# A normalized tile in two VectorE operations and one of ScalarE, with the first half of three heads in program order

## The chip, the core and the metric

One core of a Trainium2 chip runs the whole program. Its engines are TensorE (matmuls; the profile calls it PE, its weight loads PEld), VectorE (DVE), ScalarE (ACT), GpSimd (POOL) and SyncE (SP, which here only issues DMAs). The metric is the device time of one execution in microseconds, lower is better; a time given is the median of several runs.

## What is computed

A decoder trunk of two layers on 512 tokens of width 1024, all in float32. Each layer is a token mixer (stick-breaking attention in layer 0, a state-space layer in layer 1) and a gated MLP with a causal convolution (the ffn). Ahead of each of these four, and at the end, stands a normalization that is modulated by a conditioning vector:

```python
def rms_norm(x, g):
    y = xf * lax.rsqrt(jnp.mean(xf * xf, axis=-1, keepdims=True) + EPS)
    return y * g
def modulate(h, shift, scale):
    return h * (1 + scale[:, None, :]) + shift[:, None, :]
for i in range(DEPTH):
    h = modulate(rms_norm(x, norm_mix[i]), sh1, sc1)
    x = x + g1 * mixer(h)                    # attention, then state space
    h = modulate(rms_norm(x, norm_ffn[i]), sh2, sc2)
    x = x + g2 * conv_ffn(h, ...)
```

## The kernel before

x lies transposed in SBUF: 8 tiles (k = 0 to 7) of 128 channels by 512 tokens. A matmul in full precision is made of three products (`mm3`): each operand is split in a high part and a low part (hH and hL of the activations, w_h and w_l of the weights), and the products are hH by w_h (L171), hL by w_h (L174) and hH by w_l (L175), all three into one PSUM bank. A weight tile of 128x1024 is split by ScalarE (L165, high) and VectorE (L166, low).

A tile of h is made in `norm_tile`: VectorE multiplies x by rbc, the reciprocal root mean square of each token, broadcast over the partitions (L308, into t); ScalarE makes hH = b + a t (L315, rounded to the matmul's type) and the same once more without rounding into u (L317); VectorE subtracts, hL = u - hH (L321). a and b are columns: one number for each channel. The same function makes tiles 1 to 7 in attention's values stretch (`pinned`, 512 columns, rbc copied into SBUF as rb) and the tiles of three heads.

A head (`head_mm`) is the first part of ffn 0, of the state-space layer and of ffn 1: four banks of output (`hd`; in an ffn, gate and value of units 0 and 1, in the state-space layer u0 to u3) are filled tile by tile while h is being made. For tiles 0 to 5 the tokens are taken in two halves of 256 columns, first all six tiles of the first half, then all six of the second; tiles 6 and 7 are full. The first half can start when the residuals of the first half are complete. While it runs, the tail of the output projection before it finishes the second half: the residual add (L355), its square (L244) and the sum (acc, L245). The second half's statistic (`rstd_stat`: four matmuls L266, ScalarE's root L270, five small VectorE operations L271 to L275 and two diagonal tiles dg, L283) is traced ahead of tile 1's third bank (HEADS = (1, 2)), and its broadcast (`rstd_bc`, L288, a matmul of dg by ones into the bank rbc) ahead of tile 3's third bank (HEADB = (3, 2)).

The order on each engine is set when the program is built: a planner takes instructions that are ready by its own estimate, the earlier traced first, unless an edge says otherwise. `pe_pin` (`keep_in_program_order`) puts an instruction behind the one traced just before it on its engine; it has no say on what is traced later. In `mm3`, `pinned` pins the first of the three products. The products of a bank keep their order among themselves. In the heads the products are not pinned, statistic and broadcast are. `behind_head` queues the splits of the next four weight tiles behind the operations of the head's tiles 4, 8, 11 and 13 (HEADW, places in the list `pin["head"]`).

Behind an ffn's head come the units: for each, two banks of 24 products of 512 columns, then the convolution (ScalarE L459, VectorE L461 twice, for gate and value), Silu (L471), the product (L473) and the split of the result (L477, L478). These follow one another in a written order (`follow`). In ffn 0 VectorE and GpSimd also prepare the tables of the state-space layer in between. In the state-space layer, behind the head, u0 to u3 are copied (L1286) and written to DRAM (sU) and read back in another layout (u); the matmuls pv (L1280) need that.

Of the kernel before, what the change touches and what calls it, by code (L numbers as in the profile page):

```python
# [7 lines left out]
F32 = mybir.dt.float32  # L8
# [3 lines left out]
AF = mybir.ActivationFunctionType  # L12
ALU = mybir.AluOpType
# [3 lines left out]
P = 128  # L17
T = 512
D = 1024
KD = D // P  # L20
# [64 lines left out]
def trunk(tc, I, out, tap=lambda *a: None):  # L85
    with ExitStack() as ctx:
        _trunk(ctx, tc, I, out, tap)


def _trunk(ctx, tc, I, out, tap):  # L90
    nc = tc.nc
    V, S, G, PE, SP = nc.vector, nc.scalar, nc.gpsimd, nc.tensor, nc.sync

    def pool(name, bufs=1, **kw):
        return ctx.enter_context(tc.tile_pool(name=name, bufs=bufs, **kw))
# [5 lines left out]
    np_ = pool("np")  # L101
# [9 lines left out]
    x = [xp.tile([P, T], F32, tag=f"x{k}", name=f"x{k}") for k in range(KD)]  # L111
# [25 lines left out]
    pin = {"head": []}  # L137
# [31 lines left out]
    def mm3(ps, lhs, rhs, start, stop, pinned=False):  # L169
        (ah, al), (bh, bl) = lhs, rhs  # L170
        ins = PE.matmul(ps, ah, bh, start=start, stop=False)  # L171
        if pinned:
            tc.keep_in_program_order(ins)
        PE.matmul(ps, ah, bl, start=False, stop=False)  # L174
        PE.matmul(ps, al, bh, start=False, stop=stop)  # L175
# [7 lines left out]
    def wk(w, k):  # L183
        if isinstance(w[0], list):
            return tuple(half[k // 4][:, k % 4 * P:(k % 4 + 1) * P] for half in w)
        return w[0][:, k * P:(k + 1) * P], w[1][:, k * P:(k + 1) * P]
# [20 lines left out]
    def mcol(l, v, j):  # L207
        return l * 48 + v * 8 + j
# [24 lines left out]
    HALF = (slice(0, T // 2), slice(T // 2, T))  # L233
# [44 lines left out]
    def rstd_stat(R, cr, pinned=False):  # L278
        t0, t1 = cr.start // P, cr.stop // P
        dg = R["dg"]  # L280
        y = rstd_y(R, cr, pinned)
        for i in range(t0, t1):
            ins = V.tensor_scalar(dg[:, i * P:(i + 1) * P], ident, y[:, i - t0:i - t0 + 1], None, ALU.mult)  # L283
        return ins

    def rstd_bc(R, cr, pl, pinned=False):
        bc = bank(pl, "rbc")
        ins = PE.matmul(bc[:, cr], ones, R["dg"][:, cr], start=True, stop=True)  # L288
        if pinned:
            pe_pin(ins)  # L290
        R["bc"][cr.start] = bc
# [7 lines left out]
    def half_cols(ap, cr):  # L299
        return ap.rearrange("p (j c) -> p j c", j=CH)[:, :, cr.start // CH:cr.stop // CH]  # L300

    def norm_tile(h, k, bc, a, b, cr=FULL, pinned=False, first=None, mid=None):
        n = cr.stop - cr.start
        t = np_.tile([P, T], F32, tag="nt1", bufs=2, name="nt1")[:, :n]
        u = np_.tile([P, T], F32, tag="nt2", bufs=1, name="nt2")[:, :n]
        for part in HALF if cr == FULL and isinstance(bc, dict) else (cr,):
            src = bc[part.start] if isinstance(bc, dict) else bc
            pin["nt"] = V.tensor_tensor(t[:, part.start - cr.start:part.stop - cr.start], x[k][:, part], src[:, part], ALU.mult)  # L308
        hh, hl = h[0][k][:, cr], h[1][k][:, cr]
        hf = hh.bitcast(F32)  # L310
        keep = pe_pin if pinned else lambda ins: None
        keep(pin["nt"])
        if first:
            first()
        act = S.activation(hh, t, AF.Identity, bias=b[:, k:k + 1], scale=a[:, k:k + 1])  # L315
        keep(act)
        aff = S.activation(u, t, AF.Identity, bias=b[:, k:k + 1], scale=a[:, k:k + 1])  # L317
        keep(aff)
        if mid:
            mid()  # L320
        dve = V.tensor_tensor(hl, u, hf, ALU.subtract)  # L321
        keep(dve)
        pin["head"].append([act, aff, dve])


    def head_mm(R, h, a, b, hd):
        pin["head"] = []
        todo = [(k, HALF[0]) for k in range(HEADK)] + [(k, HALF[1]) for k in range(HEADK)] + [(k, FULL) for k in range(HEADK, KD)]
        made = 0
        for n, (k, cr) in enumerate(todo):  # L330

            while made < (min(n + 3, HEADK) if cr == HALF[0] else n + 1):
                norm_tile(h, todo[made][0], R["bc"], a, b, todo[made][1])
                made += 1
            for q, (w, ps) in enumerate(hd):
                if cr == HALF[0] and (k, q) == HEADS:
                    rstd_stat(R, HALF[1], True)
                if cr == HALF[0] and (k, q) == HEADB:
                    rstd_bc(R, HALF[1], mm, True)
                mm3(ps[:, cr], wk(w, k), (h[0][k][:, cr], h[1][k][:, cr]), k == 0 and cr.start == 0, k == KD - 1)  # L340

    @contextmanager
    def behind_head(pins=None):
# [82 lines left out]
    def ffn(l, R, prep=None, last=None, hook=lambda: None):  # L426
# [4 lines left out]
        with ExitStack() as fc:  # L431
# [61 lines left out]
            for gi, gn in enumerate(GROUPS):  # L493
# [4 lines left out]
                if gi == 0:  # L498
                    hx, ws = pin["hw"]
                    hd = [(q, s, ws[2 * q + s], bank(name=f"up{l}_{q}_{s}")) for q in range(2) for s in range(2)]  # L500
                    head_mm(R, h, a, b, [q[2:] for q in hd])
                    hx.close()
                    for q in range(4):
                        with behind_head(pin["head"][HEADW[q]]):
                            split_next(False)
                    pin["prep"] = [pin["split"]]
                    for q in range(2):
                        gs.append(unit_out(q, q, [hd[2 * q + s][3] for s in range(2)]))
                    i = 2
                    step = prep(fc) if prep else (lambda: None)  # L510
# [31 lines left out]
    def attention(acc):  # L542
        with ExitStack() as av_, ExitStack() as ac:
# [139 lines left out]
            for k in range(1, KD):  # L683
                def mid():
                    nxt[0] = high(k + 1) if k < KD - 1 else None
                    pe_pin(V.tensor_tensor(w[1], raws[k], w[0].bitcast(F32), ALU.subtract))
                    if k < KD - 1:
                        gv(1, k + 1)

                nxt = [None]  # L690
                gv(0, k)
                norm_tile(h, k, rb, a, mod[:, 0:KD], FULL, True, None, mid)
                if k + 2 < KD:
                    raws[k + 2] = loads(k + 2)
                prods(k, w)
                w = nxt[0]
# [542 lines left out]
    def ssm(R):  # L1239
# [3 lines left out]
        with ExitStack() as zc:  # L1243
# [3 lines left out]
            with ExitStack() as sc:  # L1247
# [20 lines left out]
                hx, ws = pin["hw"]  # L1268
                hd = [(ws[bi], bank(name=f"u{bi}")) for bi in range(4)]
                head_mm(R, h, a, b, hd)  # L1270
                hx.close()
                sp = sc.enter_context(tc.tile_pool(name="ssm", bufs=1, reuse_waits="tile"))
# [211 lines left out]
    b = mod[:, mcol(2, 0, 0):mcol(2, 0, 0) + KD]  # L1484
# [154 lines left out]
```

## Time and profile before

| | us |
|---|---|
| median of 3 runs (1175.2 to 1176.14) | 1175.74 |
| the profiled execution | 1175.82 |
| its span, first to last instruction | 1174.0 |
| TensorE busy | 1158.9 |
| VectorE busy | 857.7 |
| ScalarE busy | 563.5 |

The profile is of one execution. Busy is the time in which an engine has an instruction of its own under way; matmuls are pipelined, a row lasts longer than its turn, and the turn is seen by the distance to the start of the next row. The three heads lie at 262.6 to 290.8 (ffn 0), 634.7 to 658.9 (state space) and 801.6 to 829.8 us (ffn 1); attention's values stretch is 21 to 65 us.

### The profile page before, as it was taken

Reading aid. Unit: us, or ns where it says so; the run is one execution under the profiler, and the core shown is the slowest. Engines: PE = TensorE matmul, PEld = TensorE weight load, DVE = VectorE, ACT = ScalarE, POOL = GpSimd, SP = SyncE. Lnnn points to the kernel's source line nnn. Section 1 sums busy time; section 2 is a strip of 40 time slices with the busy share of each in tenths; the row PEclk is TensorE's granted clock in tenths of the full one; section 3 lists DMA queues with packets and bytes.
Section 4 is the critical chain, followed back from the end, with each engine's and each line's share of the span. In section 5 each row is a group of like instructions: output and inputs, shape, how many; then the busy total and the mean of one; then the engine's idle time right before and its main releaser. Section 6 shows DMA issues by size and latency. Waiting matters only on the chain.

```text
span 1174.0 us, 16592 instructions
## 1 busy us (share of the span) xinstructions
PE 1158.9 (99%) x6242; PEld 964.2 (82%) x6242; DVE 857.7 (73%) x1311; ACT 563.5 (48%) x896; POOL 270.8 (23%) x278
## 2 busy tenths in 40 slices
PE   8999999999999999999999999999999999999997
PEld 7887777699788888888889888789888888888887
DVE  6968888775998666787757599887598378744555
ACT  6756667456453244413346477647443144422443
POOL 2001110000298799979800000000000000000003
PEclk8999999999999999999999999999999999999999
DMA  8873656331267858797756598671176357432322
GB/s 320 292 264 116 192 162 195 111 123 55 78 189 268 247 167 252 198 292 253 230 151 223 149 353 293 207 255 50 49 231 217 107 153 184 133 123 73 92 69 72
DMA packets 91618, 211.01 MB, mean 180 GB/s; under 512 B 19601, under 2 KB 37905, under 8 KB 91538
## 3 DMA queue, kind: packets, MB, share of 16 engines
q1 hardware_dynamic: 78562, 191.08, 51.0%
q0 software_dynamic: 4656, 16.78, 4.5%
q10 hardware_dynamic: 8320, 2.10, 0.8%
q8 instruction: 49, 0.80, 0.3%
q14 instruction: 31, 0.25, 0.1%
HBM read 188.68 MB, written 21.24 MB: 179 GB/s over the span
## 4 chain that ended last, share of the span: by engine, by line
PE 78%; DVE 7%; issue 7%; DMA 5%; ACT 2%; POOL 1%; SPq 1%; POOLq 0%; DVEq 0%; ACTq 0%
PE up L171 13%; PE up L174 13%; PE up L175 13%; PE dn L171 6%; PE dn L174 6%; PE dn L175 6%; DMA wg<-in_w_modT_dram 3%; PE u L174 1%; PE u L171 1%; PE u L175 1%; PE wo L171 1%; PE wos L174 1%; PE wo L175 1%; PE wo L174 1%; PE wos L175 1%
## 5 line engine op out<-in xcount | busy, mean ns | idle before, releaser
L171 PE MATMUL up<-hH,up_h 128*128 128x512 f32 x640 | 249.7, 391 | 0.3 <-DVE ca L461 0.3
L175 PE MATMUL up<-hH,up_l 128*128 128x512 f32 x640 | 249.3, 390 | 0.3 <-DVE up_l L166 0.3
L174 PE MATMUL up<-hL,up_h 128*128 128x512 f32 x640 | 249.3, 390 | 0.0
L461 DVE SCALAR_TENSOR_TENSOR ca<-up,small,ca 128x511 f32<-128x511 f32 (+1 forms) x176 | 131.6, 748 | 120.7 <-ACT ca L459 117.6
L171 PE MATMUL dn<-gH,dn_h 128*128 128x512 f32 (+1 forms) x394 | 145.0, 369 | 0.0
L198 DVE SCALAR_TENSOR_TENSOR wg<-wg,cact 128x1024 f32<-128x1024 f32 x96 | 121.4, 1281 | 31.7 <-DMA wg<-in_w_modT_dram 31.6
L174 PE MATMUL dn<-gL,dn_h 128*128 128x512 f32 (+1 forms) x394 | 144.5, 367 | 0.0
L175 PE MATMUL dn<-gH,dn_l 128*128 128x512 f32 (+1 forms) x394 | 144.4, 366 | 0.0
L171 PEld LDWEIGHTS up<-hH,up_h 128*128 128x128 f32 x640 | 120.1, 188 | 26.5 <-issue 1.5
L175 PEld LDWEIGHTS up<-hH,up_l 128*128 128x128 f32 x640 | 120.1, 188 | 25.9 <-DVE up_l L166 1.1
L174 PEld LDWEIGHTS up<-hL,up_h 128*128 128x128 f32 x640 | 120.1, 188 | 24.4
L459 ACT ACTIVATE ca<-up,small 128x512 f32<-128x512 f32 x88 | 68.2, 775 | 149.5 <-PE up L175 149.5
L1511 POOL TENSOR_SCALAR xa<-x,Anorm_out 128x256 f32<-128x256 f32 x7 | 5.7, 818 | 570.3 <-DVE x L355 570.3
L165 ACT ACTIVATE up_h<-up_r 128x1024 fp32r<-128x1024 f32 x80 | 84.2, 1052 | 75.3 <-PE dn L174 58.1
L166 DVE TENSOR_TENSOR up_l<-up_r,up_h 128x1024 fp32r<-128x1024 f32 x80 | 116.3, 1454 | 5.4 <-ACT up_h L165 4.5
L355 DVE SCALAR_TENSOR_TENSOR x<-dn,mod,x 128x512 f32<-128x512 f32 (+1 forms) x55 | 37.4, 680 | 71.4 <-PE dn L175 71.4
L171 PEld LDWEIGHTS dn<-gH,dn_h 128*128 128x128 f32 x394 | 74.3, 189 | 12.9 <-issue 0.6
L174 PEld LDWEIGHTS dn<-gL,dn_h 128*128 128x128 f32 x394 | 74.3, 189 | 12.1
L175 PEld LDWEIGHTS dn<-gH,dn_l 128*128 128x128 f32 x394 | 74.3, 189 | 12.1
L165 ACT ACTIVATE dn_h<-dn_r 128x1024 fp32r<-128x1024 f32 (+1 forms) x48 | 46.7, 982 | 46.2 <-PE dn L174 38.5
L166 DVE TENSOR_TENSOR dn_l<-dn_r,dn_h 128x1024 fp32r<-128x1024 f32 (+1 forms) x48 | 61.6, 1283 | 0.8 <-ACT dn_h L165 0.5
L477 ACT ACTIVATE gH<-gm 128x512 fp32r<-128x512 f32 x44 | 27.1, 616 | 67.3 <-DVE gm L473 67.3
(349 smaller groups left out, 2311.0 us busy)
## 6 DMA issues: line engine op xcount, KB each, us to landing
up_r<-in_w_up_dram SPq DMA_DIRECT2D x80, 512.0 KB
wg<-in_w_modT_dram SPq DMA_DIRECT2D x71, 512.0 KB
dn_r<-in_w_down_dram SPq DMA_DIRECT2D x32, 512.0 KB
wg<-in_w_modT_dram POOLq DMA_DIRECT2D x25, 512.0 KB, 4.0
wgs<-in_w_modT_dram SPq DMA_DIRECT2D x16, 512.0 KB
dn_r<-in_w_down_dram SPq DMA_DIRECT2D x16, 384.0 KB
wv_r<-in_w_v_dram SPq DMA_DIRECT2D x8, 512.0 KB
wk_r<-in_w_qk_dram SPq DMA_DIRECT2D x8, 512.0 KB
```

The costliest lines, as they stand in the source:

```text
L165: order("S", lambda: S.activation(wh[:, :n], raw[:, :n], AF.Copy))
L166: pin["split"] = order("V", lambda: V.tensor_tensor(wl[:, :n], raw[:, :n], wh[:, :n].bitcast(F32), ALU.subtract))
L171: ins = PE.matmul(ps, ah, bh, start=start, stop=False)
L174: PE.matmul(ps, ah, bl, start=False, stop=False)
L175: PE.matmul(ps, al, bh, start=False, stop=stop)
L198: mul = lambda: V.scalar_tensor_tensor(w, w, 1.0, cact, ALU.mult, ALU.mult, accum_out=raw[:, col:col + 1])
L355: add = lambda: V.scalar_tensor_tensor(xs, pv, gate, xs, ALU.mult, ALU.add)
L459: follow("S", lambda: S.activation(ca, ps, AF.Identity, bias=small[:, cb:cb + 1], scale=tapw[2]))
L461: follow("V", lambda: V.scalar_tensor_tensor(ca[:, q:], ps[:, :T - q], tapw[2 - q], ca[:, q:], ALU.mult, ALU.add))
L477: follow("S", lambda: S.activation(gh, m, AF.Copy))
L1511: G.tensor_scalar(xa[k], x[k][:, cb], a[:, k:k + 1], 0.0, ALU.mult, ALU.add)
```

## The change

The gain a goes into VectorE's first operation, which becomes t = x a rbc; ScalarE makes hH = t + b only; VectorE's second operation adds b itself, hL = (t + b) - hH. The tile u and ScalarE's second operation go. In the heads, the products of the first half (tiles 0 to 5) are traced with `pinned`.

```diff
     def norm_tile(h, k, bc, a, b, cr=FULL, pinned=False, first=None, mid=None):
         n = cr.stop - cr.start
         t = np_.tile([P, T], F32, tag="nt1", bufs=2, name="nt1")[:, :n]
-        u = np_.tile([P, T], F32, tag="nt2", bufs=1, name="nt2")[:, :n]
         for part in HALF if cr == FULL and isinstance(bc, dict) else (cr,):
             src = bc[part.start] if isinstance(bc, dict) else bc
-            pin["nt"] = V.tensor_tensor(t[:, part.start - cr.start:part.stop - cr.start], x[k][:, part], src[:, part], ALU.mult)
+            pin["nt"] = V.scalar_tensor_tensor(t[:, part.start - cr.start:part.stop - cr.start], x[k][:, part], a[:, k:k + 1], src[:, part], ALU.mult, ALU.mult)
         hh, hl = h[0][k][:, cr], h[1][k][:, cr]
-        hf = hh.bitcast(F32)
         keep = pe_pin if pinned else lambda ins: None
         keep(pin["nt"])
         if first:
             first()
-        act = S.activation(hh, t, AF.Identity, bias=b[:, k:k + 1], scale=a[:, k:k + 1])
+        act = S.activation(hh, t, AF.Identity, bias=b[:, k:k + 1])
         keep(act)
-        aff = S.activation(u, t, AF.Identity, bias=b[:, k:k + 1], scale=a[:, k:k + 1])
-        keep(aff)
         if mid:
             mid()
-        dve = V.tensor_tensor(hl, u, hf, ALU.subtract)
+        dve = V.scalar_tensor_tensor(hl, t, b[:, k:k + 1], hh.bitcast(F32), ALU.add, ALU.subtract)
         keep(dve)
-        pin["head"].append([act, aff, dve])
+        pin["head"].append([act, dve])
...
-                mm3(ps[:, cr], wk(w, k), (h[0][k][:, cr], h[1][k][:, cr]), k == 0 and cr.start == 0, k == KD - 1)
+                mm3(ps[:, cr], wk(w, k), (h[0][k][:, cr], h[1][k][:, cr]), k == 0 and cr.start == 0, k == KD - 1, cr == HALF[0])
```

## Rows read from the trace of the kernel before

**Rows 1.** The page, part 1: busy time, share of the span, instructions.

```profile
PE 1158.9 (99%) x6242; PEld 964.2 (82%) x6242; DVE 857.7 (73%) x1311; ACT 563.5 (48%) x896; POOL 270.8 (23%) x278
```

**Rows 2.** Stretches: length, busy of PE, PEld, DVE, ACT, POOL, clock, DMA.

```profile
21.00:62.00 41.00, 41.00 (x185) 33.76 (x184) 38.37 (x58) 30.36 (x53) 0.00 (x0) 1.00 0.85 286
262.50:290.80 28.30, 28.30 (x196) 26.06 (x195) 16.07 (x40) 18.45 (x32) 0.18 (x2) 1.00 0.20 57
```

**Rows 3.** Timeline of TensorE, head 1: start, duration, instruction, how many merged.

```profile
262.59 0.64 PE L171 MATMUL up<-hH,upo_h 128*128 128x256 f32 x4
263.06 0.28 PE L174 MATMUL up<-hL,upo_h 128*128 128x256 f32 x1
...
265.94 0.50 PE L266 MATMUL stat<-ones,acc 128*128 128x1 f32 x4
...
270.17 0.59 PE L288 MATMUL rbc<-dg,ones 128*128 128x256 f32 x2
...
272.49 0.39 PE L171 MATMUL up<-hH,up_h 128*128 128x512 f32 x1
272.87 0.39 PE L174 MATMUL up<-hL,upo_h 128*128 128x256 f32 x1
273.09 0.28 PE L175 MATMUL up<-hH,upo_l 128*128 128x256 f32 x1
```

**Rows 4.** Timeline of ScalarE and TensorE behind head 1, ffn 0.

```profile
289.65 0.78 ACT L459 ACTIVATE ca<-up,small 128x512 f32<-128x512 f32 x1 [6.89 <-PE up L175]
...
307.86 0.39 PE L174 MATMUL up<-hL,up_h 128*128 128x512 f32 x1
308.09 0.39 PE L175 MATMUL up<-hH,up_l 128*128 128x512 f32 x1
308.75 0.47 PE L171 MATMUL up<-hH,up_h 128*128 128x512 f32 x1 [0.27 <-DVE ca L461]
...
309.79 0.50 PE L175 MATMUL up<-hH,up_l 128*128 128x512 f32 x1 [0.34 <-DVE up_l L166]
```

**Rows 5.** Timeline of all engines, start of head 2.

```profile
634.65 0.73 PE L171 MATMUL u<-hH,win_h 128*128 128x256 f32 x4
634.76 0.48 DVE L355 SCALAR_TENSOR_TENSOR x<-dn,mod,x 128x256 f32<-128x256 f32 x1 [0.46 <-PE dn L175]
...
635.16 0.41 DVE L321 TENSOR_TENSOR hL<-nt,hH 128x256 fp32r<-128x256 f32 x1
...
635.63 0.38 PE L174 MATMUL u<-hL,win_h 128*128 128x256 f32 x1 [0.24 <-DVE hL L321]
```

**Rows 6.** Timeline of all engines behind head 2, state-space layer.

```profile
657.68 1.09 ACT L1286 ACTIVATE ut<-u 128x512 f32<-128x512 f32 x2 [3.24 <-PE u L175]
...
668.50 1.15 PE L1280 MATMUL pv<-u,pB 128*64 128x64 f32 x32 [1.30 <-issue]
```

**Rows 7.** ScalarE's groups by form: count, busy, mean ns of one, idle before.

```profile
L317 ACT ACTIVATE nt<-nt,mod,Anorm_ffn 128x256 f32<-128x256 f32 x24 | 14.3, 596 | 0.3 <-DVE hL L321 0.3
L315 ACT ACTIVATE hH<-nt,mod,Anorm_ffn 128x256 fp32r<-128x256 f32 x24 | 14.2, 590 | 4.5 <-DVE nt L308 4.5
...
L244 ACT ACTIVATE sq<-x 128x256 f32<-128x256 f32 x25 | 10.4, 416 | 24.4 <-DVE x L355 22.5 <-DVE acc L245 1.8
```

**Rows 8.** VectorE's groups by form.

```profile
L308 DVE TENSOR_TENSOR nt<-x,rbc 128x256 f32<-128x256 f32 x48 | 18.9, 415 | 2.1 <-PE rbc L288 2.0
...
L321 DVE TENSOR_TENSOR hL<-nt,hH 128x256 fp32r<-128x256 f32 x36 | 15.3, 424 | 7.8 <-ACT nt L317 7.6
...
L355 DVE SCALAR_TENSOR_TENSOR x<-dn,mod,x 128x256 f32<-128x256 f32 x14 | 6.8, 482 | 5.2 <-PE dn L175 5.2
```

**Rows 9.** Timeline of VectorE, head 1, from the statistic to the split.

```profile
267.26 0.43 DVE L321 TENSOR_TENSOR hL<-nt,hH 128x256 fp32r<-128x256 f32 x1
...
267.98 0.48 DVE L283 TENSOR_SCALAR dg<-consts,ny 128x128 f32<-128x128 f32 x2
268.38 1.22 DVE L166 TENSOR_TENSOR up_l<-up_r,up_h 128x1024 fp32r<-128x1024 f32 x1
```

## The prediction

> **What bounds the kernel now.** I read the share of busy time on the page first: TensorE is busy for 1158.9 of 1174.0 us, VectorE for 73%, ScalarE for 48% [rows 1]. So work taken off ScalarE is worth nothing by itself; only a place where TensorE waits can give time back. The table of stretches comes next. In the stretch of the values (21 to 62) TensorE is busy for all 41.00 us, and in the first head (262.5 to 290.8) for all 28.30 [rows 2]. But a matmul's row is longer than its turn: in the head products of 256 columns show 0.28 us and start 0.118 us apart (four from 262.59, the next at 263.06: 0.47/4 [rows 3]), and those of 512 columns show 0.39 and start 0.23 apart (307.86 to 308.09 [rows 4]). Waits shorter than that overlap are therefore no idle time, and I looked for them by the distance of starts, in the timeline of TensorE. Four places are left that this change can touch:
>
> - In heads 1 and 3, at the start of the second half: 272.49 to 272.87 is 0.38 for a product that takes 0.23, and 272.87 to 273.09 is 0.22 for one of 0.12 [rows 3]. That is 0.25 us; head 3 shows the same pattern, so 0.5 for both.
> - In head 2, at its first tile: TensorE starts four products at 634.65 (0.47 of work) and the next one at 635.63, waiting for hL, which VectorE starts at 635.16 because the residual of the tail, 634.76, stands ahead of it [rows 5]. That is 0.98 - 0.47 = 0.51.
> - In the first ffn, 18 us behind head 1: 308.09 to 308.75 instead of 0.23, released by VectorE's convolution (L461, a bank that is not free), and 308.75 to 309.79 for two products (0.46), released by VectorE's weight split [rows 4]. That is 0.43 + 0.58 = 1.0 us. VectorE is behind here since ScalarE could take up the first unit only at 289.65 [rows 4], when the head's first bank was complete.
> - At the first pv of the state-space layer: 1.30 us idle at 668.50, on u0, which goes through DRAM from the copy at 657.68 on [rows 6].
>
> All four together are 3.3 us, and that is about the most that can be had.
>
> **Part 1, the tile of h.** ScalarE loses L317 in each tile: 596 ns in a half tile, 36 of these, and 13 full ones. Its other operation keeps a bias column and loses the scale column; its price lies between 416 ns (the square of the same size, without columns) and 590 as now [rows 7]. I take 500. VectorE's two operations become three-operand forms with a column. The nearest row is the residual L355 of the same size, 482 ns, against 415 and 424 for the forms that go [rows 8]. So each costs between nothing and 67 ns more; I take 67 and 58, as L355 has two tensors and a column like the new ones. Over 55 first and 49 second operations that is at most 55 x 67 + 49 x 58 ns = 6.5 us on VectorE. In the values stretch 7 tiles add 0.9 us to 38.37 of 41.00 [rows 2]; TensorE stays the longer one, so I cost it at nothing, up to +0.1 if the first tile, which TensorE meets at once, is late.
>
> [...]
>
> What counts is the latency from the broadcast to hL. Now: 415 + 590 + about 500 (L317 starts 0.5 behind L315) + 424, some 1.93 us; then: 482 + 500 + 482, some 1.46. hL follows hH after 0.5 instead of 0.95 us. The tile t is now held until hL is made, not until L317 has read it, but both its writer and that reader are VectorE's, so no wait between engines is added. A new wait is that VectorE's first operation needs the gain column, made by ScalarE; in the heads it is made long before. In the values stretch the order written out in the code makes the column one tile ahead, so I cost it at nothing; queued behind that operation would be the split of wv and the next row of the modulation.
>
> **Part 2, the pins.** A pinned instruction is ordered behind the one traced just before it on its engine. With the first product of each bank pinned in the first half, and the three products of a bank in order already, the first half runs bank by bank: statistic ahead of tile 1's third bank, broadcast ahead of tile 3's third. Now the statistic runs at 265.94, behind tile 2's first products, and the broadcast at 270.17, behind all of tile 4 [rows 3]. Then: 18 products from 262.59 give 264.7 for the statistic, and 24 more with its own 0.37 give 267.9 for the broadcast, 2.2 us sooner. The first half ends at about 271.8 (72 x 0.118 + 0.37 + 0.35 behind 262.59; the last two are what statistic and broadcast take out of the row of products now), while hL of the second half's first tile can be there at 267.9 + 0.35 + 0.3 + 1.46 = 270.0. So the waits at 272.5 go; no matmul and no DMA is added or moved between queues.
>
> What TensorE now can't do is pass a late tile: it needs hL one product behind hH, not four, so the 0.45 us gained on hL pays for 0.35 us of sooner need. In head 2 that decides: hH(0) at 634.6, hL at 635.1 if VectorE takes it ahead of the residual, 635.7 if behind. Against 635.6 now: -0.4 or +0.2, and I take 0.
>
> **Where the stall of the ffn goes.** In head 1 TensorE runs 196 instructions in 28.3 us [rows 2], of which the head has 174 (144 half products, 24 full, 4 and 2 for statistic and broadcast). Some 20 are products of unit 2, of 512 columns, the first at 272.49 [rows 3], put where hL was expected late. They take 20 x 0.23 = 4.6 us ahead of the head's last tiles. With hL sooner the order need not hold them, the first unit's bank is complete some 4 us before 289.65, and VectorE's chain of convolutions, which is 1.0 us late 18 us on, begins that much sooner. I take the whole 1.0; if the 20 stay, nothing. What is late next is VectorE's preparation work for the state-space layer, which fills its gaps, and the same total of matmuls.
>
> **At pv.** If the last tile of head 2 runs bank by bank instead of four first products ahead, u0 is complete three products (0.7 us) sooner and the wait of 1.30 shrinks as much; the full tiles are not pinned, so I take 0.3 of 0 to 0.7.
>
> **The sum.** The profiled execution took 1175.82 (span 1174.0 and 1.8 around it); the median of three is 1175.74. Heads 1 and 3: -0.4 of 0.5. Head 2: 0 (-0.4 to +0.2). ffn: -1.0 (0 to -1.0). pv: -0.3 (0 to -0.7). Values: 0 (up to +0.1). Stalls in a strict first half: +0.2 (0 to +1.3 per head, below). Together -1.5: **1174.3 us**.
>
> **Rivals.** *Only the heads tighten* (the 20 products stay, or the pins order nothing that matters): -0.4, 1175.4. For it: the second half and the full tiles are not pinned; against it: the shorter chain holds everywhere. *All four places go*: -0.5 - 0.4 - 1.0 - 0.7 = -2.6, and 0.5 more where products are denser than now: 1172.7. For it: each has hL or the first unit's start as its cause.
>
> *VectorE is late at the broadcast, and TensorE waits with nothing to put in.* Now dg ends 2.52 us behind the statistic (267.98 + 0.48 - 265.94 [rows 3, 9]), with one hL among it. In the strict order TensorE is at the broadcast 3.2 us behind the statistic: 0.7 to spare. The weight split of 1.22 us stands right behind dg now [rows 9], and its ScalarE half comes sooner, too; if it goes ahead of dg, with two tile operations of 0.4 each, dg is 1.22 + 0.8 - 0.7 = 1.3 us late, in three heads 3.9, and the ffn's stall stays: 1179.5 with the 0.2 of the sum in it. It decides from the point where dg ends over 3.2 us behind the statistic.
>
> [...] VectorE is busy for 16.07 of 28.30 us in head 1 [rows 2], so the rows don't call it saturated; the rival needs only a wrong order.
>
> **Chances.** Forecast 0.45, only the heads 0.28, all four 0.17, late broadcast 0.10. A measurement of this kernel tells a change of about 0.2% (2.35 us) from none: faster is below 1173.4, slower above 1178.1. Faster: 0.17 and the lower end of the forecast, 0.10, so 0.27; slower 0.10; the same 0.63. The range takes the all-four case with a little below it (1172.3) and the heads' case with one head stalling by 1.3 (1176.7).
>
> **What would show it.** In the trace after: starts in the first half in the order L171, L174, L175, bank by bank; the statistic near 264.7 and the broadcast near 267.9, with no start more than 0.2 late there; no products of unit 2 ahead of tile 7; the first convolution near 285.5; no wait for VectorE near 308; the wait ahead of pv below 1.3. Wrong it would be if TensorE waits for dg or acc in a head, or if the order of unpinned work elsewhere changes by more than the waits named here.

## The result, and the profile after

The changed kernel takes 1180.88 us (median of five, 1178.6 to 1182.39) against 1175.37 for the kernel before; the ratio is 1.0045, with a 95% interval of 1.0030 to 1.0059. It is 5.3 us slower, where I had forecast 1.5 us faster. The profiled execution has a span of 1179.1 us, 5.1 above the 1174.0 of before.

Line numbers behind ScalarE's operation (L314) are three lower than before (hL is L318, the scan L795, the residual L352). The page's first part says that the work went where I had said, out of ScalarE (563.5 to 532.8) and a little into VectorE (857.7 to 859.7 [rows 1]):

```profile
PE 1161.1 (98%) x6242; PEld 965.6 (82%) x6242; DVE 859.7 (73%) x1311; ACT 532.8 (45%) x847; POOL 271.0 (23%) x278
```

The groups by form, with the mean ns of one behind the comma, give the new prices, to be read beside [rows 7, 8]:

```profile
L314 ACT ACTIVATE hH<-nt,mod 128x256 fp32r<-128x256 f32 x36 | 17.1, 503 | 23.4 <-DVE nt L308 22.3 <-PE wo L175 1.0
L318 DVE SCALAR_TENSOR_TENSOR hL<-nt,mod,hH 128x256 fp32r<-128x256 f32 x36 | 16.4, 482 | 1.1 <-ACT hH L314 1.1
L308 DVE SCALAR_TENSOR_TENSOR nt<-x,Anorm_ffn,rbc 128x256 f32<-128x256 f32 x32 | 14.1, 478 | 2.1 <-PE rbc L288 1.9
L308 DVE SCALAR_TENSOR_TENSOR nt<-x,Amix,rb 128x512 f32<-128x512 f32 x7 | 5.3, 754 | 0.8 <-ACT Amix L583 0.8
```

So the loss is not in the prices: 482 and 500 were forecast, 478 to 482 and 503 are measured. The last row has something that the old tile didn't have, 0.8 us in which VectorE waits for the gain column Amix.

The list of TensorE's waits over the whole span (total us, how many, the longest) shows three places:

```profile
PE t L807 <- DVE om L795: 2.6, 5, 1.0
...
PE rbc L288 <- DVE dg L283: 1.4, 3, 0.6
...
PE stat L266 <- DVE acc L245: 0.8, 2, 0.4
PE u L174 <- DVE hL L318: 0.7, 1, 0.7
```

Before, the second did not occur, the third was 0.3 in one, the fourth 0.2, and the first was this:

```profile
PE t L810 <- DVE om L798: 0.7, 2, 0.5
```

These lists count idle time only; by the distance of starts, TensorE lost 1.8, 2.3 and 1.9 us in the heads against 0.9, 1.2 and 0.9 before, counted from a head's first product on (each sum is the excess over 0.227 us for a product of 512 columns and 0.118 for 256, the distances measured, and over 0.063 for 128, an estimate: half the step of 0.109 between those two, taken off 0.118; the heads have none of 128). Summed in the same way over attention (100 to 244), it lost 17.4 us against 14.0. For the 146 transposes in this stretch the estimate is too low: they start 0.109 us apart, before and after, so that some 6.7 us of each sum (146 x 0.046) are no loss; the 3.4 between them stay. But single executions differ much there: the kernels below whose attention is as before lose 12.3 to 16.9. The wait for the scans (om) is the clearer sign: it is 2.6 here, 3.0 in e1, and at most 1.3 in every other run.

**Attention.** VectorE at the end of the values stretch, after:

```profile
50.10 0.75 DVE L308 SCALAR_TENSOR_TENSOR nt<-x,Amix,rb 128x512 f32<-128x512 f32 x1 [0.36 <-ACT Amix L583]
...
55.41 0.75 DVE L308 SCALAR_TENSOR_TENSOR nt<-x,Amix,rb 128x512 f32<-128x512 f32 x1 [0.47 <-ACT Amix L583]
...
57.21 1.22 DVE L166 TENSOR_TENSOR wk_l<-wk_r,wk_h 128x1024 fp32r<-128x1024 f32 x1
58.35 1.22 DVE L166 TENSOR_TENSOR wq_l<-wq_r,wq_h 128x1024 fp32r<-128x1024 f32 x1
59.48 0.74 DVE L318 SCALAR_TENSOR_TENSOR hL<-nt,mod,hH 128x512 fp32r<-128x512 f32 x1
...
77.22 0.69 DVE L728 TENSOR_TENSOR vn<-vn,vs 128x512 f32<-128x512 f32 x1 [1.31 <-DMA vs<-sV]
...
88.60 5.83 DVE L795 TENSOR_TENSOR_SCAN om<-om,maskb 128x128 f32<-128x128 f32 x8
```

Before, the last hL of the stretch stood ahead of the split wq_l:

```profile
56.73 0.69 DVE L321 TENSOR_TENSOR hL<-nt,hH 128x512 fp32r<-128x512 f32 x1 [0.51 <-ACT nt L317]
57.68 1.23 DVE L166 TENSOR_TENSOR wq_l<-wq_r,wq_h 128x1024 fp32r<-128x1024 f32 x1 [0.26 <-ACT wq_h L165]
...
85.71 5.84 DVE L798 TENSOR_TENSOR_SCAN om<-om,maskb 128x128 f32<-128x128 f32 x8
```

From the first tile on (25.25 before, 25.88 after) hL is 2.1 us later and the scan 2.3. Between them lies a chain. ScalarE's next weight split waits for its load (3.34 us, to 60.93; before 0.79, to 58.43). VectorE's copies of the values out of PSUM stand behind these splits (from 65.94 on, before 63.05). The values are then written to DRAM, read back one row shifted (vs) and subtracted (first at 77.22, before 74.78), and only then do the scans get VectorE. The chain has a little slack: in e2 (below), whose values stretch is as before, hL comes 30.67 us behind the first tile, 0.8 sooner than before, and the scan only 0.2 sooner. At some 114 us TensorE has used up its lead and its transposes wait for the scans.

**The heads.** Head 1 after, in the timelines of TensorE, ScalarE and VectorE, in order of time:

```profile
269.04 0.60 PE L266 MATMUL stat<-ones,acc 128*128 128x1 f32 x4
269.16 1.04 ACT L165 ACTIVATE up_h<-up_r 128x1024 fp32r<-128x1024 f32 x1
270.23 1.23 DVE L166 TENSOR_TENSOR up_l<-up_r,up_h 128x1024 fp32r<-128x1024 f32 x1 [0.46 <-ACT up_h L165]
270.50 0.24 ACT L270 ACTIVATE nsd<-stat,epst 128x2 f32<-128x2 f32 x1
...
272.62 0.48 DVE L283 TENSOR_SCALAR dg<-consts,ny 128x128 f32<-128x128 f32 x2
273.16 0.70 PE L288 MATMUL rbc<-dg,ones 128*128 128x256 f32 x2 [0.56 <-DVE dg L283]
```

The weight split (ScalarE's 1.04, VectorE's 1.23 us) now stands ahead of the root nsd and of dg; before it stood right behind dg (268.38 [rows 9]). It is queued behind tile 4's operations, and with the short tile these come ahead of the statistic's. dg ends at 273.10, 4.06 us behind the statistic, against 2.52 before (3.79 and 4.00 in heads 2 and 3). The broadcast starts 0.84 behind the product ahead of it (272.32), where 0.12 is its turn.

### The profile page after: what moved, and what is told of

The parts are those of the page before. It is cut to its first block, busy times and chain, and to the rows that moved or that the text cites. A ratio compares the mean times of both kernels' runs of the same rounds, so it can differ in the third digit from the quotient of the medians.

```text
span 1179.1 us, 16546 instructions
## 1 busy us (share of the span) xinstructions
PE 1161.1 (98%) x6242; PEld 965.6 (82%) x6242; DVE 859.7 (73%) x1311; ACT 532.8 (45%) x847; POOL 271.0 (23%) x278
## 4 chain that ended last, share of the span: by engine, by line
PE 79%; issue 7%; DVE 6%; DMA 4%; ACT 2%; POOL 1%; SPq 1%; POOLq 0%; DVEq 0%; ACTq 0%
PE up L171 13%; PE up L174 13%; PE up L175 13%; PE dn L171 6%; PE dn L174 6%; PE dn L175 6%; DMA wg<-in_w_modT_dram 2%; PE u L171 1%; PE u L174 1%; PE u L175 1%; PE wo L171 1%; PE wos L174 1%; PE wo L175 1%; PE v L171 1%; PE wo L174 1%
## 5 line engine op out<-in xcount | busy, mean ns | idle before, releaser
L175 PEld LDWEIGHTS up<-hH,up_l 128*128 128x128 f32 x640 | 120.1, 188 | 25.1
L166 DVE TENSOR_TENSOR up_l<-up_r,up_h 128x1024 fp32r<-128x1024 f32 x80 | 113.6, 1420 | 5.9 <-ACT up_h L165 5.0
L352 DVE SCALAR_TENSOR_TENSOR x<-dn,mod,x 128x512 f32<-128x512 f32 (+1 forms) x55 | 37.5, 681 | 73.4 <-PE dn L175 73.3
L474 ACT ACTIVATE gH<-gm 128x512 fp32r<-128x512 f32 x44 | 27.1, 617 | 68.2 <-DVE gm L470 68.2
```

Source lines behind the costliest of these rows:

```text
L166: pin["split"] = order("V", lambda: V.tensor_tensor(wl[:, :n], raw[:, :n], wh[:, :n].bitcast(F32), ALU.subtract))
L352: add = lambda: V.scalar_tensor_tensor(xs, pv, gate, xs, ALU.mult, ALU.add)
L474: follow("S", lambda: S.activation(gh, m, AF.Copy))
```

## The experiments

Each was timed in turns with the kernel before. Single runs of one kernel lie up to 8 us apart, so the interval of each ratio stands here; us are the ratio less 1, times 1175.4. In the kernels that hold both tile functions the lines behind `norm_tile` are 23 or 24 higher.

**The change in its parts.** First the new tile in one of its two places each, with the old one in the other, and the pins alone.

```diff
+    def norm_tile(h, k, bc, a, b, cr=FULL, pinned=False, first=None, mid=None):
+        f = norm_tile_new if pinned else norm_tile_old     # e1; e2 and e3 the other way round
+        f(h, k, bc, a, b, cr, pinned, first, mid)
...
-                mm3(..., k == 0 and cr.start == 0, k == KD - 1)
+                mm3(..., k == 0 and cr.start == 0, k == KD - 1, cr == HALF[0])     # e3 and e4
```

> The new tile only in attention's values stretch (tiles 1 to 7), the heads and their products as before. Theory (VectorE paces that stretch: every period of a tile grows from 4.63 to 4.75 us, and the first operation also waits for the gain column): the last hL of the stretch comes 2 us or more later than at 56.73, the first scan of attention 1.5 to 3 us later than at 85.71, TensorE then waits for the scans between 100 and 244, and the time is 2.5 to 4 us above before: 1178 to 1179.4. Rival (the waits in attention were a chance of the loads in that one execution): first scan within 0.5 us of 85.71, time within 0.6 of before's 1175.4.

Measured: 1.0024 (1.0012 to 1.0036), +2.8 us. The timelines of ScalarE and VectorE, and in a fence of its own TensorE's waits from 100 to 244:

```profile
53.03 1.07 ACT L591 ACTIVATE wv_h<-wv_r 128x1024 fp32r<-128x1024 f32 x1 [2.02 <-DMA wv_r<-in_w_v_dram]
54.30 1.06 ACT L165 ACTIVATE wk_h<-wk_r 128x1024 fp32r<-128x1024 f32 x1 [0.21 <-DMA wk_r<-in_w_qk_dram]
55.58 0.39 ACT L609 ACTIVATE Amix<-mod,small 128x1 f32<-128x1 f32 x1
56.00 0.75 DVE L330 SCALAR_TENSOR_TENSOR nt<-x,Amix,rb 128x512 f32<-128x512 f32 x1 [1.72 <-ACT Amix L609]
60.08 0.74 DVE L340 SCALAR_TENSOR_TENSOR hL<-nt,mod,hH 128x512 fp32r<-128x512 f32 x1
88.78 4.72 DVE L821 TENSOR_TENSOR_SCAN om<-om,maskb 128x128 f32<-128x128 f32 x7
```

```profile
PE t L833 <- DVE om L821: 3.0, 5, 1.7
```

The first scan is at 88.78 again and TensorE waits 3.0 us for scans. With the change's own trace these are two executions, so it is no chance of one. The gain column of tile 7 stands on ScalarE behind two weight splits, wv_h and wk_h, which wait 2.02 and 0.21 us for their loads, and VectorE idles 1.72 us for it.

> The new tile only in the three heads, no pins, values stretch as before. Theory (the stretch from 21 to 244 is untouched; in the heads the weight split now goes ahead of the diagonal tiles on VectorE, but TensorE, not pinned, puts other products in while it waits; the stall at 308 and the one ahead of pv go): 1 to 2.5 us below before, 1173 to 1174.5. Rival (the order that VectorE gets from the shorter tile costs the heads as much without pins as with them): 0.5 to 1.5 above before, 1176 to 1177, with over 0.5 us of TensorE waiting for dg in each head.

Measured: 1.0041 (1.0026 to 1.0057), +4.8 us. The theory falls: without pins the new tile in the heads costs far more, not less. The rival falls too: TensorE waits 1.1 us in each head for hH of the second half, and nowhere in the heads for dg. e12 comes back to it.

> The new tile in the three heads and the pinned first half, values stretch as before: the change without its part in attention. Theory (two separate losses): attention as before, each head loses about 1 us to acc and dg, the stalls of the ffn and of pv are gone (-1.4 and -1.5): 0 to 1.5 above before, 1175.4 to 1177. Rival (all of the loss comes from the heads, and the waits in attention are chance): 4 to 5.5 above before, 1179.4 to 1181.

Measured: 1.0016 (1.0005 to 1.0027), +1.9 us, a little over the forecast; TensorE's list has the same 1.4 for dg, 0.8 for acc and 0.7 for hL as after, and 0.7 for the scans as before. e1 and e3 together are 4.7 of the 5.3 us: two separate losses.

> The old tile everywhere, only the products of the first half pinned. Theory (it is the shorter tile that brings the weight split ahead of dg; with the old tile the split stays behind dg): TensorE waits for dg under 0.3 us in each head, time 0 to 1.5 above before from waits for hL, 1175.4 to 1177. Rival (the pins alone make TensorE meet the statistic and the broadcast too early): 0.5 us or more of waiting for dg or acc in each head, time 2 to 4 above before.

Measured: 0.9987 (0.9976 to 0.9998), -1.5 us, faster than forecast. dg ends 3.02 us behind the statistic in head 1 (264.90 + 0.48 - 262.36) and in no head does TensorE wait for it. So the pins by themselves are a small gain, with an interval that just leaves out 1, and of the two kernels and all variants this and e11 are the fastest.

**The split's place in the heads.** Two kernels, one that moves the split back with the new tile, one that moves it forward with the old; two more, e11 and e12, ask what else counts in the heads.

```diff
# e5; u_units, in the state-space layer, gets the same
-                    rstd_stat(R, HALF[1], True)
+                    pin["dgi"] = [rstd_stat(R, HALF[1], True)] + [R["nsd"]]
...
-                        with behind_head(pin["head"][HEADW[q]]):
+                        with behind_head(pin["head"][HEADW[q]] + (pin["dgi"] if q == 0 else [])):
```

> As e3_heads_new_pin (new tile in the heads, pinned first half), with one edge more: the first weight split behind a head is queued behind the root and the diagonal tiles of the second half's statistic. Theory (the split, ScalarE's 1.04 and VectorE's 1.23 us, went ahead of root and dg because the shorter tiles finish before the statistic): the waits for dg of 0.56 to 0.72 us in each of the three heads are gone, 1.2 to 2 us below e3's 1177.6: 1175.6 to 1176.4. Rival (dg is late because the statistic itself waits for acc, or because the new operations are longer): the waits stay over 0.3 us in each head, time within 0.5 of 1177.6.

Measured: 0.9993 (0.9979 to 1.0006), -0.8 us; by the ratios that is 2.7 below e3, more than forecast (the two were timed on two chips). Head 1, TensorE and VectorE:

```profile
265.49 0.61 PE L266 MATMUL stat<-ones,acc 128*128 128x1 f32 x4
...
267.71 0.48 DVE L283 TENSOR_SCALAR dg<-consts,ny 128x128 f32<-128x128 f32 x2
268.11 1.22 DVE L166 TENSOR_TENSOR up_l<-up_r,up_h 128x1024 fp32r<-128x1024 f32 x1
...
268.89 0.59 PE L288 MATMUL rbc<-dg,ones 128*128 128x256 f32 x2
```

dg ends 2.70 us behind the statistic, the broadcast starts 3.40 behind it, in its turn. The wait for dg is gone from the list; no other edge was changed. The statistic still waits for acc, 0.4 us in head 3.

> As e4_pin_only (old tile everywhere, pinned first half), but the first weight split of each head is queued behind tile 3 instead of tile 4 (HEADW 3 for 4), so that it stands ahead of the statistic's operations on VectorE, as it does with the new tile. Theory (the place of the split makes dg late, whatever the tile): TensorE waits for dg 0.5 to 1.5 us in each head, 1.5 to 3.5 us above e4's 1173.9: 1175.5 to 1177.5. Rival (the split finds a gap on VectorE with the old tile): waits for dg under 0.3 us, time within 0.6 of e4.

 The edit is `HEADW = (3, 8, 11, 13)` for `(4, 8, 11, 13)` in e4.

Measured: 1.0015 (1.0004 to 1.0025), +1.8 us, 3.3 above e4 (by the ratios; the two were timed on two chips):

```profile
266.43 1.22 DVE L166 TENSOR_TENSOR up_l<-up_r,up_h 128x1024 fp32r<-128x1024 f32 x1 [0.20 <-ACT up_h L165]
...
268.62 0.48 DVE L283 TENSOR_SCALAR dg<-consts,ny 128x128 f32<-128x128 f32 x2
...
269.16 0.48 PE L288 MATMUL rbc<-dg,ones 128*128 128x256 f32 x1 [0.85 <-DVE dg L283]
```

The statistic is at 264.84, dg ends 4.26 behind it, as late as in the changed kernel, with the old tile. It is the split's place that makes dg late, whatever the tile.

> As e5_split_behind_dg, with the statistic of the second half six products later (HEADS 2, 0 for 1, 2) and its broadcast six later (HEADB 4, 0 for 3, 2). Theory (what is left in heads 1 and 3 is the statistic's wait for acc, 0.3 to 0.45 us each, and behind tile 4's start there is room): no wait for acc or dg, 0.5 to 1 us below e5. Rival (the second half's tiles come later by the same 0.7 us and TensorE waits there): the same or up to 1 us above e5.

Measured: 0.9989 (0.9976 to 1.0002), -1.3 us. The interval of it and that of e5 overlap, so that the move helps is not shown; in its profile heads 1 and 3 have no wait for acc or dg left and lose 0.6 us each against e5's 0.9 and 1.2, but the statistic ahead of head 2 waits 0.8 for acc, and waits of 1.4 in all for the table pB come behind head 2.

> As e2_heads_new (new tile in the heads, no pins), with the first weight split behind the diagonal tiles as in e5. Theory (without pins too it is the split ahead of the statistic that makes the broadcast late: TensorE waited 1.1 us for hH behind it in each head): dg ends under 3 us behind the statistic, the waits for hH behind the broadcast shrink below 0.4 us each, 2 to 4 us below e2: 1 to 3 above before. Rival (the order of TensorE's products without pins is the cause, the broadcast stands late however early dg is): as e2, 4 to 5.5 above before.

Measured: 1.0036 (1.0022 to 1.0050), +4.2 us: the rival. Head 1, TensorE and VectorE:

```profile
266.03 0.50 PE L266 MATMUL stat<-ones,acc 128*128 128x1 f32 x4
...
267.72 0.49 DVE L283 TENSOR_SCALAR dg<-consts,ny 128x128 f32<-128x128 f32 x2
...
269.94 0.59 PE L288 MATMUL rbc<-dg,ones 128*128 128x256 f32 x2
271.65 0.74 PE L171 MATMUL up<-hH,upo_h 128*128 128x256 f32 x4 [1.12 <-ACT hH L336]
```

dg is ready at 268.21, 2.18 us behind the statistic; in e2's head 1 it was 2.17, so there the split's place was not what cost. The statistic comes 5.14 us behind the head's first product (in e5 2.44), and the broadcast 1.73 behind dg, because the unpinned order has it behind all 72 products of the first half, which it need not wait for. Then the first half is used up, and TensorE waits 1.12 us for the second half's first tile. e5 differs from this kernel in the pins alone and is 5.1 us faster by the ratios. So the pins are what keeps statistic and broadcast early when the tiles are short.

**The values stretch.** The two things that e1's rows show, a late gain column and a late last tile, are mended; and the added work alone is put in.

```diff
# e7, on e1
                 def mid():
-                    nxt[0] = high(k + 1) if k < KD - 1 else None
                     pe_pin(V.tensor_tensor(w[1], raws[k], w[0].bitcast(F32), ALU.subtract))
                     if k < KD - 1:
                         gv(1, k + 1)
+                    nxt[0] = high(k + 1) if k < KD - 1 else None
...
-        order("S", lambda: S.activation(wh[:, :n], raw[:, :n], AF.Copy))
-        pin["split"] = order("V", lambda: V.tensor_tensor(wl[:, :n], raw[:, :n], wh[:, :n].bitcast(F32), ALU.subtract))
+        with behind_head() if name == "wq0" else ExitStack():
+            order("S", lambda: S.activation(wh[:, :n], raw[:, :n], AF.Copy))
+            pin["split"] = order("V", lambda: V.tensor_tensor(wl[:, :n], raw[:, :n], wh[:, :n].bitcast(F32), ALU.subtract))
# e6, on the kernel before; e9 has a tile of [P, 16] and writes 8 columns of it
+        if pinned:
+            keep(V.tensor_copy(np_.tile([P, 8], F32, tag="dum", bufs=1, name="dum"), x[k][:, 0:8]))
```

> As e1_values_new (new tile in the values stretch alone), but ScalarE makes the gain column of the next tile ahead of its weight split, and the first q split is queued behind tile 7's hL, as it stood before: the new tile without the wait for the gain and without the late last tile. Theory A (three parts: pace 0.8, gain wait 0.8, order 0.4 and more): last hL about 1 us later than at 56.73 and not 3.3, first scan about 1 us later than at 85.71, time 0.5 to 1.5 above before. Rival C (the longer operations alone do it): first scan still 2.5 us later or more, time as e1, 2 to 3.5 above.

Measured: 1.0005 (0.9995 to 1.0016), +0.6 us. VectorE's timeline, and TensorE's waits from 100 to 244:

```profile
52.68 0.74 DVE L331 SCALAR_TENSOR_TENSOR nt<-x,Amix,rb 128x512 f32<-128x512 f32 x1
55.61 0.74 DVE L341 SCALAR_TENSOR_TENSOR hL<-nt,mod,hH 128x512 fp32r<-128x512 f32 x1
84.78 5.83 DVE L822 TENSOR_TENSOR_SCAN om<-om,maskb 128x128 f32<-128x128 f32 x8
```

```profile
PE t L834 <- DVE om L822: 0.7, 2, 0.5
```

This execution reached its first tile early (24.16), so distances are compared: from the first tile to the last hL it takes 31.45 us, before 31.48, in e1 34.40; to the first scan 60.62, before 60.46, in e1 63.10. The period of a tile is 4.75 us (43.17 to 47.93 for two first operations) against 4.63, and most of this growth disappears in a wait that the last tile had before (0.51 us for ScalarE's second operation). The first scan comes 0.1 to 0.4 us later than in the kernels that keep this stretch as before (60.22 to 60.54). So of e1's 2.8 us 2.2 go with the two places in the order; they were changed together, and what each is worth stays open. The 0.6 left for the longer operations is not told from nothing.

> The kernel before with one small VectorE copy (128x8, about 0.14 us) behind the first operation of each of the tiles 1 to 7 in the values stretch: the added work of the new tile (2 x 0.07 us) without its other effects. Theory A (VectorE paces the stretch, so the added work alone is carried through): period of a tile 4.63 + 0.14, last hL and first scan 1 us later, time 0.5 to 1.5 above before's 1175.4; the rest of e1's 2.8 us is the wait for the gain column and the order of the splits. Rival B (TensorE paces the stretch, the added work is hidden): first scan within 0.3 us of 85.71, time within 0.4 of before. Rival C (the added work is the whole of e1's loss): first scan 2.5 us later or more, time 2 to 3.5 above.

Measured: 1.0048 (1.0033 to 1.0063), +5.6 us, and yet no theory held whole: the period of a tile is 4.70 us, but the first scan, from the first tile, is at 60.43 and the wait for scans 0.7, both as before (rival B), while the time is beyond every forecast. What had grown are products far away, by form:

```profile
L171 PE MATMUL dn<-gH,dn_h 128*128 128x512 f32 x310 | 122.5, 396 | 0.0
L175 PE MATMUL dn<-gH,dn_l 128*128 128x512 f32 x310 | 122.5, 395 | 0.0
L174 PE MATMUL dn<-gL,dn_h 128*128 128x512 f32 x310 | 122.4, 395 | 0.0
```

Before it is 390, 389 and 389 ns, and the starts lie 0.233 us apart instead of 0.227. By the distance of starts these 930 products take 6.0 us more in sum; the products of 256 columns that read the same tiles (84 of each kind) take no more (279 to 286 ns, before 283 to 289). That is about the whole loss.

> As e6_values_0p14_per_tile (the kernel before with a 0.16 us copy in each of seven tiles), but the copy's scratch tile takes 64 bytes of a partition instead of 32. In e6 the products that read the ffn's hidden tiles started 0.233 us apart instead of 0.227, some 7 us in sum, and attention lost nothing. Theory (e6's loss is the place of the tiles behind the scratch tile, not the work): products at 0.227 us again, period of a tile about 4.70 us, first scan within 1 us of before's, time within 1 us of before's. Rival (the added VectorE work itself costs the 5.8 us): time 1181 to 1183 again.

Measured: 1.0015 (1.0000 to 1.0029), +1.8 us, between the two.

```profile
L171 PE MATMUL dn<-gH,dn_h 128*128 128x512 f32 x310 | 121.9, 394 | 0.0
L175 PE MATMUL dn<-gH,dn_l 128*128 128x512 f32 x310 | 121.5, 392 | 0.0
L174 PE MATMUL dn<-gL,dn_h 128*128 128x512 f32 x310 | 120.7, 389 | 0.0
```

The added work is the same as in e6, only the scratch tile is larger. The products are less slow: the 930 take 2.0 us more than before, where in e6 it was 6.0. Less that, e6 and e9 lie 0.4 and 0.2 us below before, so the added work costs nothing that these runs can tell. In the changed kernel the same products start 0.227 us apart, as before, so this is no part of the 5.3 us.

**The whole change, mended.** The edits of e5 and e7 on the changed kernel:

> The whole change with three places in the order mended: the gain column ahead of the weight split and the q split behind tile 7's hL (as in e7), the first weight split of a head behind the diagonal tiles (as in e5). Theory (the 5.3 us are the sum of these three places, and the operations themselves cost next to nothing): the sum of e5's -0.5 and e7's +0.7, so within 1 us of before, 1174.5 to 1177. Rival (the longer VectorE operations cost something wherever they stand): 2 us or more above before.

Measured: 1.0004 (0.9991 to 1.0017), +0.5 us, 4.8 below the change by the ratios. So nearly all of the 5.3 us are three places in the order of the instructions, and what is left is not told from nothing. But what is left of the idea is no gain, and it stays 2.0 us behind the pins alone (e4), with intervals that just overlap. In its profile the statistic still waits for acc in head 3 (0.4 us), which it does not in the kernel before.

## Why the prediction was wrong

**The values stretch at nothing, up to +0.1: the step that failed first.** It cost 2.8 us. I saw that VectorE was busy for 38.37 of 41.00 us [rows 2], saw that TensorE was busy for all of it, and stopped there. A narrower window would have warned me: between 25.25 and 53.05 us VectorE is busy for all 27.80 us, so there any wait of its own makes it late. I even named the new wait, for the gain column, and costed it at nothing because "the order written out in the code makes the column one tile ahead". So it does, but it puts the column behind a weight split: the code makes the high part of wv's next tile (`high(k + 1)`) ahead of the column (`gv(1, k + 1)`), and that split waits for its load (2.02 us for tile 7 in e1). At the last tile the planner puts a second split, wk_h, between. The old first operation did not read the gain, so the same order cost nothing. And I looked only for TensorE's waits inside the stretch. What VectorE is late with there is handed on through a chain of copies and DMAs to a stretch where TensorE does wait for VectorE, the scans of attention, which I had not looked at.

**The late broadcast, at 0.10: the rival that came.** Its mechanism is what happened, step by step: the split goes ahead of dg, and dg ends later than TensorE gets to the broadcast. The deciding point was given as 3.2 us behind the statistic; where nothing waits the broadcast comes 3.3 (e4, 265.66 - 262.36) and 3.4 us behind it (e5), and in the changed kernel dg ends 4.06 behind it. The price was too high, 1.3 us per head for 0.72 in head 1 (273.16 - 272.32 - 0.12), and the stall of the ffn didn't stay. What failed is its chance: I held that the split needs "a wrong order", though the edit that shortens the tile is what brings tile 4's operations, and the split queued behind them, ahead of the statistic. That this rival's 1179.5 lies near the 1180.88 measured is luck: it had the whole loss in the heads, and without the values stretch (e3) the loss is 1.9 us.

**Stalls in a strict first half, +0.2: the term that was too small.** By the distance of starts the three heads lose 3.0 us more than before (6.0 against 3.0), where this term and those of the heads made -0.2 together. What follows goes through them.

**Heads 1 and 3, -0.4 of 0.5: replaced.** The gap at the second half's start is gone, but the wait for dg takes its place, and the statistic waits for acc: by the distance of starts 0.3 us in head 1 and 0.5 in head 3, where before it waited in neither. (The list's other wait for acc, 0.4, stands ahead of head 2, where it was 0.3 before.) In head 1 the last sum into acc starts at 268.56, 0.57 behind the end of its square, with two tile operations ahead of it on VectorE; before it was 0.13.

**Head 2, 0 (-0.4 to +0.2).** hL of the first tile stands behind the residual here too:

```profile
638.29 0.38 PE L171 MATMUL u<-hH,win_h 128*128 128x256 f32 x1
638.43 0.48 DVE L352 SCALAR_TENSOR_TENSOR x<-dn,mod,x 128x256 f32<-128x256 f32 x1 [0.34 <-PE dn L175]
638.83 0.48 DVE L318 SCALAR_TENSOR_TENSOR hL<-nt,mod,hH 128x256 fp32r<-128x256 f32 x1
639.36 0.39 PE L174 MATMUL u<-hL,win_h 128*128 128x256 f32 x1 [0.69 <-DVE hL L318]
```

The gap is 1.07 - 0.12 = 0.95 us against 0.51 before [rows 5]: +0.4, beyond the upper end. The wait for hL was foreseen (1.07 us from the first product, 1.1 in the prediction's working); what the term left out is that strict order has one product to put in and not four, 0.35 us less.

**The stall of the ffn, -1.0: the stall went, and more than forecast.** Between 306 and 318 no wait is left, and the stretch of 291 to 350 loses 0.2 us by the distance of starts, before 1.6. Fewer products of unit 2 stand ahead of the head's last ones (9, before 20; none was forecast). The first convolution comes 25.1 us behind the head's first product (291.65 - 266.59), before 27.1; 2 us and not 4 sooner. In e4, with the pins and the old tile, the stretch loses 0.8; in e3 and e5 0.1, but also in e8, with the old tile and the earlier split. So the pins give half of it, and either the tile or the earlier split the rest. In e2 the stretch loses 0.9, though the first convolution is as late as before; that the sooner convolution alone is the cause is not shown.

**The wait ahead of pv, -0.3: gone, but not by the change.** In e1, where the heads are as before, pv starts 9.44 us behind the copy, with no wait; in the profiled execution of before it was 10.82 [rows 6]:

```profile
661.69 1.09 ACT L1309 ACTIVATE ut<-u 128x512 f32<-128x512 f32 x2 [3.25 <-PE u L175]
...
671.13 1.15 PE L1303 MATMUL pv<-u,pB 128*64 128x64 f32 x32
```

In e6, e7 and e9 there is no such wait either. It was that execution's delay of the transfer through DRAM: ScalarE waited 4.84 us there for its first writes to DRAM, in e1 3.19. I had taken a wait seen once for a property of the kernel.

**The prices.** They were right, and so was the row chosen for them. L308, which reads the broadcast from PSUM, took 478 ns, L318, which reads SBUF alone, 482, the price of the row they were taken from.

What is not settled: whether the added VectorE work costs anything up to some 2 us (e7's interval reaches 1.9, e10's 2.0), how the loss in the values stretch divides between its two places, and how e4's 1.5 us divide, since single executions of one kernel differ by more.

## What to carry to other kernels

When an operation gets shorter, list what is queued behind it by an edge and what that will now overtake; a weight split that goes ahead of a short step on the critical chain can cost more than the shorter operation gives (2.7 us from e3 to e5). Follow lateness of an engine that is "hidden" out of its stretch to the next place where somebody waits for that engine, through DMAs too. A wait that is seen in one execution alone is not yet something that a change can win.

## What the runs showed of the hardware

With a scratch tile of 32 bytes of a partition, taken from a pool that others lie behind (e6), the products of 512 columns that read the ffn's hidden tiles gH and gL (as moving operand) start 0.233 us apart instead of 0.227 (1044.6 to 1046.1 us); the mean granted clock of the profiled execution was 0.994 in e6 and 0.995 before. With 64 bytes (e9) those of gL are as before (389 ns in the rows) and those of gH in between (392 and 394). Both kernels have the same copies, so it is the size of the tile that makes the difference between them. The products of 512 columns of the ffn that read h (up, 640 of each kind) took 389 to 391 ns in e6 and in e9, before 390 and 391. That the tiles moved by those bytes is inferred from the pool's order; the trace doesn't show addresses. It cost some 6 of 1175 us in e6 and 2 in e9, and would have been booked on the experiment's cause, had the products not been looked at.
